# Five of eight pairs of the up projection as products of sums, and low parts by accumulating transfers from HBM, in one encoder layer

## The chip, the cores and the metric

The kernel runs on one core of one Trainium2 chip. The metric is device time in microseconds (us) of one execution. The five engines of the core each run their own list of instructions: TensorE (PE: matmuls, with weight loads shown apart as PEld), VectorE (DVE), ScalarE (ACT), GpSimd (POOL) and SyncE (SP), which here only issues loads. GpSimd issues some transfers too. TensorE writes to PSUM, everything else lives in SBUF, and weights come from HBM by DMA.

## The reference, cut to what matters

One layer of an encoder on 256 tokens of width 2048, all in float32: two kinds of attention side by side with one input and one output projection, cross attention to 256 memory tokens, a SwiGLU with 5632 hidden columns, and a last RMSNorm.

```
h = rms_norm(x, g_mix);   proj = h @ w_in              # MLA and differential attention
x = x + concat([out_mla, out_diff]) @ w_out
x = x + cross_attention(rms_norm(x, g_xattn), rms_norm(mem, g_mem)) @ w_xo
hf = rms_norm(x, g_ffn)
x = x + (silu(hf @ w_gate) * (hf @ w_up)) @ w_down     # w_gate, w_up: 2048 x 5632
return rms_norm(x, g_final)
```

The change concerns the line with `w_gate`, `w_up` and `w_down`.

## The kernel before

**A float32 product as three matmuls.** Each operand is split into a high part (`.h`, the value cast to the reduced type fp32r) and a low part (`.l`, the rest, also fp32r). A product is high × high, high × low and low × high. Of a weight block of 128 × 1024, ScalarE makes the high part by a cast (tile `wh`), and VectorE the low part by a subtract (tile `wl`). Both tiles have rings of four buffers (`w_tile`, L602).

**Pairs.** The depth of a product is taken in pairs of 2 × 128 rows, so hf's 2048 are eight pairs. `wide_project` (L644) computes 256 tokens × 1024 columns: it walks over the pairs in a given order, and for each loads 1 MB of weights into one of three `wraw` buffers (`pair_raw`, L596, issued by SP). A pair has one of two kinds:

- `P`, plain: 2 depths × 2 token halves × 2 column halves × 3 = 24 matmuls of 512 columns, into four accumulators `acc` in PSUM. VectorE makes two low parts of 1024 columns.
- `W`, products of sums (the Strassen–Winograd form for a 2 × 2 block): 7 products × 3 = 21 matmuls, into the accumulators and into four more PSUM banks `q1`, `q5`, `q6`, `q7`. It needs sums of weight blocks, which VectorE writes to the tile `tsum` (one 1024-wide, two 512-wide operations), and the split of each: `b11` and `b21` from `wraw`, `t13` and `t24` from `tsum` (`t24` in single tiles `wh2` and `wl2`). It also needs sums of the activations, the `forms` of `summed_pair` (L627), made once.

`GU_KINDS` (L38) says which pairs are which in gate and up, `G_ORDER` and `U_ORDER` (L46) in which order they are walked.

**Carried low parts.** For a block named in `CARRIED` (L42: pair 0, second block) `split_blocks` (L608) makes the low part without VectorE: ScalarE writes the negated block to `wl`, and the cast to `wh`; then a DMA that GpSimd issues adds the raw block from `wraw` to `wl`.

```
nc.scalar.activation(w.l, src, AF.Copy, scale=-1.0)
nc.scalar.copy(out=w.h, in_=src)
nc.gpsimd.dma_start(out=w.l, in_=src, accum_op=ALU.add)
```

**Stages.** The FFN has a chunk of 512 hidden columns (`narrow_chunk`, L1258) and five wide chunks of 1024 (`wide_chunk`, L1270). A wide chunk is gate by `wide_result`, silu on ScalarE, up by `wide_result`, the multiply on VectorE and the transposes. After the first wide chunk, the third and the fifth stand two down projections each (`wide_add`, L736), whose accumulators start from the residual `x_res`. When the pairs of sums of a down projection are done, `leave` (L744) stores the four sums made of the `q` banks in tiles `left` out of a ring of five (`nat`).

**What sets the order.** The kernel's text only records operations. A planner (`Plan`, L186) with a table of costs (`cost`, L252) puts each engine's operations in an order. In the FFN the matmuls keep the order in which they were recorded (`strict`, L1308 and below), and tiles of the pool `wp` are placed in program order (`Held.queued`, L128). Since one place in the planner emits every operation, all instructions bear the line L232; tiles tell them apart.

Of the kernel before, what the change touches and what calls it, by code (L numbers as in the profile page):

```python
# [10 lines left out]
F32 = mybir.dt.float32  # L11
F32R = mybir.dt.float32r
# [24 lines left out]

GU_KINDS = "PPWPWPWW"  # L38

DN_CARRIED = ((1, 1),)  # L40

CARRIED = ((0, 1),)  # L42

NARROW_KINDS, NARROW_ORDER = "PPWPWPPP", (0, 1, 3, 2, 5, 4, 6, 7)

G_ORDER, U_ORDER = (0, 2, 1, 4, 3, 6, 7, 5), (0, 2, 1, 4, 3, 6, 7, 5)  # L46

# [75 lines left out]
class Held:  # L123


    def __init__(self, pool, shape, args):
        self.pool, self.args, self.real = pool, args, None
        self.queued, self.ahead = pool.name == "wp" and pool.plan.strict, None  # L128
        self.size, self.whole = int(np.prod(shape[1:])), pool.space is not None
        self.ops, self.past, self.opened, self.old, self.end = [], [], [], None, 0.0  # L130
# [329 lines left out]
def encoder_block(tc: tile.TileContext, a, out):  # L460
# [183 lines left out]
    def wide_project(pairs, src, order, kinds, leave, join, closed=(0, 1), before=None, seed=None, carried=()):  # L644
# [6 lines left out]
        for n, i in enumerate(order):  # L651
# [9 lines left out]
            if i not in summed:  # L661
                w = [split_blocks(raw[:, 2 * k:2 * k + 2, :], carried=(i, k) in carried) for k in range(2)]
                for k in range(2):
                    products = []
                    for tt in range(NT):
                        for oc in range(2):

                            ends = stop or i == plain[-1] and tt == oc == 1
                            products.append((accs[tt][oc], pairs[i].at(k, tt), w[k][:, oc, :], not used[tt][oc],
                                             ends and k == 1 and oc in closed))  # L670
                            used[tt][oc] = True
                    mm_late(products, seed is not None)
# [63 lines left out]
    def wide_add(pairs, src, order, kinds, oc0, done=None, closed=(0, 1), before=None, carried=()):  # L736
# [498 lines left out]
    for oc in range(4):  # L1235
# [34 lines left out]
    def wide_chunk(c, kinds):  # L1270

        g = wide_result(x2_pairs, a["w_gate"][c], G_ORDER, GU_KINDS, CARRIED)
# [3 lines left out]
        u = wide_result(x2_pairs, a["w_up"][c], U_ORDER, GU_KINDS, CARRIED)  # L1276
        for oc in range(2):
# [132 lines left out]
def _lay_out(i):  # L1410
# [56 lines left out]
```

## Time and profile before

| | us |
|---|---|
| median of three runs | 1134.45 (1134.06 to 1134.86) |
| the profiled execution | 1134.3 |
| its span in the profile | 1132.5 |
| granted TensorE clock, mean | 0.998 |

The page gives each engine's busy time over the span; the windows view gives it for a stretch. A matmul row's length overlaps the next matmul, so the distance of two starts says more than the length. The groups of VectorE and ScalarE that the change touches, with shapes kept apart; the columns are line, engine, operation, output<-input, shapes, count, busy us, mean ns, idle us before them with what ended it:

```profile
L232 DVE TENSOR_TENSOR wl<-wraw,wh 128x1024 fp32r<-128x1024 f32 x306 | 370.8, 1223 | 72.8 <-ACT wh L232 65.9 <-PE q L232 5.3
L232 DVE TENSOR_TENSOR wl<-tsum,wh 128x1024 fp32r<-128x1024 f32 x112 | 135.2, 1217 | 1.5 <-ACT wh L232 1.4
L232 DVE TENSOR_TENSOR tsum<-tsum,wraw 128x512 f32<-128x512 f32 x124 | 85.0, 685 | 1.4
L232 ACT CAST wh<-wraw 128x1024 fp32r<-128x1024 f32 x321 | 334.9, 1053 | 208.9 <-PE acc L232 176.1 <-issue 12.5 <-PE q L232 5.6
L232 ACT ACTIVATE wl<-wraw 128x1024 fp32r<-128x1024 f32 x15 | 15.9, 1058 | 0.0
```

The last row is the 15 negated blocks of the carried low parts: five chunks, in each one for gate, one for up, and one for each of the five down projections that have them.

### The profile page before, as it was taken

What the parts mean: (1) busy time and instruction counts of PE and PEld (TensorE: products, weight loads), DVE (VectorE), ACT (ScalarE), POOL (GpSimd) and SP (SyncE); (2) the same over time, 40 slices, a digit from 0 to 9 for tenths busy, and PEclk for the clock granted to TensorE, in tenths of its full rate; (3) what the DMA queues carried; (4) which work ended last, traced back from release to release, by engine and by line L of the source; (5) the groups of instructions that cost most, each with busy time, mean ns of one, the idle gap of its engine ahead of it and who ended that gap; (6) DMA issues with size and microseconds to landing.
All of it is one profiled execution on the core that took longest, in us unless ns stands there. A gap on an engine that the chain in (4) does not pass through costs nothing.

```text
span 1132.5 us, 14766 instructions
## 1 busy us (share of the span) xinstructions
PE 1122.3 (99%) x5349; PEld 938.1 (83%) x5349; DVE 1011.5 (89%) x1375; ACT 715.3 (63%) x1014; POOL 72.1 (6%) x90
## 2 busy tenths in 40 slices
PE   9999999999999999999999999999999999999997
PEld 7899888888888888888888888888888888888886
DVE  7798778779997769999998999999989999999995
ACT  7756455467685556666675565767666665766762
POOL 5830000000000000000000000000000000000000
PEclk9999999999999999999999999999999999999999
DMA  9642444547654444666657666576575666667653
GB/s 358 258 166 110 149 149 158 207 167 267 232 211 172 153 169 161 205 216 216 209 204 231 224 217 203 212 232 210 190 236 175 241 224 201 223 218 223 229 184 114
DMA packets 37657, 230.03 MB, mean 203 GB/s; under 512 B 4560, under 2 KB 5840, under 8 KB 13264
## 3 DMA queue, kind: packets, MB, share of 16 engines
q1 hardware_dynamic: 33696, 216.60, 53.5%
q0 software_dynamic: 3024, 11.01, 4.4%
q10 hardware_dynamic: 864, 1.47, 0.4%
q8 instruction: 42, 0.69, 0.3%
q14 instruction: 31, 0.25, 0.1%
HBM read 219.11 MB, written 2.10 MB: 195 GB/s over the span
## 4 chain that ended last, share of the span: by engine, by line
PE 96%; DVE 1%; ACT 1%; issue 1%; POOL 0%; POOLq 0%; DVEq 0%; ACTq 0%
PE acc L232 73%; PE q L232 15%; PE pt L232 2%; PE psc L232 2%; PE acckv L232 1%; PE qT L232 1%; PE po L232 1%; PE kT L232 1%; PE ppt L232 1%; DVE wl L232 0%; PE wps L232 0%; ACT wh L232 0%; PE pod L232 0%; ACT e L232 0%; DVE res L232 0%
## 5 line engine op out<-in xcount | busy, mean ns | idle before, releaser
L232 ACT CAST wh<-wraw 128x1024 fp32r<-128x1024 f32 (+2 forms) x401 | 387.2, 975 | 259.7 <-PE acc L232 217.2
L232 DVE TENSOR_TENSOR wl<-wraw,wh 128x1024 fp32r<-128x1024 f32 (+2 forms) x386 | 430.3, 1125 | 80.6 <-ACT wh L232 72.2
L232 ACT CAST wh<-tsum 128x1024 fp32r<-128x1024 f32 (+1 forms) x124 | 124.2, 1011 | 54.6 <-PE acc L232 35.0
L232 DVE TENSOR_TENSOR wl<-tsum,wh 128x1024 fp32r<-128x1024 f32 (+1 forms) x124 | 143.4, 1166 | 2.2 <-ACT wh L232 1.4
L232 PE MATMUL acc<-wh,x2T_l 128*128 128x512 f32 x352 | 137.2, 390 | 0.0
L232 PE MATMUL acc<-wh,x2T_h 128*128 128x512 f32 x352 | 137.1, 389 | 0.0
L232 PE MATMUL q<-wh,forms_h 128*128 128x512 f32 x242 | 94.8, 392 | 0.6 <-ACT res L232 0.4
L232 PE MATMUL acc<-wl,x2T_h 128*128 128x512 f32 x352 | 94.4, 389 | 0.0
L232 PE MATMUL q<-wh,forms_l 128*128 128x512 f32 x242 | 94.4, 390 | 0.0
L232 PE MATMUL acc<-wh,x0T_h 128*128 128x512 f32 x224 | 88.1, 395 | 0.1
L232 PE MATMUL acc<-wl,x0T_h 128*128 128x512 f32 x224 | 88.1, 394 | 0.0
L232 PE MATMUL acc<-wh,x0T_l 128*128 128x512 f32 x224 | 87.8, 393 | 0.0
L232 DVE TENSOR_TENSOR tsum<-tsum,wraw 128x512 f32<-128x512 f32 x124 | 85.0, 685 | 1.4
L232 PE MATMUL q<-wl,forms_h 128*128 128x512 f32 x242 | 84.1, 389 | 0.0
L232 PE MATMUL acc<-wh,forms_h 128*128 128x512 f32 x208 | 81.2, 391 | 0.0
L232 PE MATMUL acc<-wh,forms_l 128*128 128x512 f32 x208 | 81.0, 389 | 0.0
L232 DVE TENSOR_TENSOR tsum<-wraw 128x1024 f32<-128x1024 f32 (+1 forms) x68 | 76.1, 1124 | 4.4 <-DMA wraw<-in_w_dn 2.2
L232 PE MATMUL acc<-wl,forms_h 128*128 128x512 f32 x208 | 78.2, 390 | 0.0
L232 PEld LDWEIGHTS acc<-wh,x2T_h 128*128 128x128 f32 x352 | 66.1, 188 | 13.7
L232 PEld LDWEIGHTS acc<-wh,x2T_l 128*128 128x128 f32 x352 | 66.1, 188 | 13.6
L232 PEld LDWEIGHTS acc<-wl,x2T_h 128*128 128x128 f32 x352 | 66.0, 188 | 13.6
L232 PE MATMUL acc<-wh,hT_l 128*128 128x512 f32 x188 | 73.4, 390 | 0.0
(363 smaller groups left out, 2095.6 us busy)
## 6 DMA issues: line engine op xcount, KB each, us to landing
wraw<-in_w_dn SPq DMA_DIRECT2D x41, 1024.0 KB, 4.8
wraw<-in_w_gate SPq DMA_DIRECT2D x40, 1024.0 KB, 4.8
wraw<-in_w_up SPq DMA_DIRECT2D x40, 1024.0 KB, 4.8
wraw<-in_w_in SPq DMA_DIRECT2D x24, 1024.0 KB, 4.9
wraw<-in_w_out SPq DMA_DIRECT2D x16, 1024.0 KB, 4.9
wraw<-in_w_gu SPq DMA_DIRECT2D x8, 1024.0 KB, 4.8
wl<-wraw POOLq DMA_DIRECT2D x15, 512.0 KB, 6.8
wraw<-in_w_in_lat SPq DMA_DIRECT2D x5, 832.0 KB, 7.0
```

The source lines that it names most:

```text
L232: getattr(getattr(self.tc.nc, engine), method)(*[made(x) for x in args], **{k: made(x) for k, x in kw.items()})
```

## The change

Each wide chunk gets its own kinds, order and list of carried blocks, the same in all five. Gate keeps four pairs of sums and its order, and carries three low parts instead of one. Up takes pair 3 as sums too, five of eight, walks 0, 2, 3, 1, 4, 6, 7, 5, and carries five low parts. x2, the input of gate and up, has forms for every pair that is `W` in any of them, so for pair 3 also; where a pair is plain, the product uses the plain blocks inside the forms. The last plain pair of x2 (pair 5) lies in tiles `odd` of its own.

A carried low part now lies in a tile `wc` of its own, a ring of two in the pool of the sums, while its high part stays in `wh`. The accumulating DMA reads the block from HBM, not from `wraw`. `tsum` becomes two tiles of two blocks, `tsum` and `tsum2`. The ring of `nat` goes from five to two, and `leave` stores its sums in the columns of the residual. Tiles in PSUM are placed in program order as well. The weights' layout in HBM follows the kinds, chunk by chunk.

```diff
-GU_KINDS = "PPWPWPWW"
...
-CARRIED = ((0, 1),)
...
-G_ORDER, U_ORDER = (0, 2, 1, 4, 3, 6, 7, 5), (0, 2, 1, 4, 3, 6, 7, 5)
+GATE_UP = [
+    (('PPWPWPWW', (0, 2, 1, 4, 3, 6, 7, 5), ((0, 1), (3, 1), (5, 1))),
+     ('PPWWWPWW', (0, 2, 3, 1, 4, 6, 7, 5), ((0, 1), (1, 1), (5, 1), (7, 0), (6, 0)))),
+] * 5
+X2_KINDS = "".join("W" if "W" in k else "P" for k in zip(NARROW_KINDS, *[p[0] for c in GATE_UP for p in c]))
...
-        self.queued, self.ahead = pool.name == "wp" and pool.plan.strict, None
+        self.queued, self.ahead = pool.name in ("wp", "pacc", "pps") and pool.plan.strict, None
...
-    def split_blocks(src, pool=None, carried=False):
-        w = w_tile(src.shape[1], pool)
-        if carried:
+    def split_blocks(src, pool=None, carried=None):
+        w = w_tile(src.shape[1], pool) if carried is None or not sum_pool else Split(
+            wp.tile([P, 1024], F32R, name="wh", tag="wh", bufs=4).rearrange("p (b c) -> p b c", b=2),
+            sum_pool[0].tile([P, 1024], F32R, name="wc", tag="wc", bufs=2).rearrange("p (b c) -> p b c", b=2))
+        if carried is not None:
             nc.scalar.activation(w.l, src, AF.Copy, scale=-1.0)
             nc.scalar.copy(out=w.h, in_=src)
-            nc.gpsimd.dma_start(out=w.l, in_=src, accum_op=ALU.add)
+            nc.gpsimd.dma_start(out=w.l, in_=carried, accum_op=ALU.add)
...
-            b11 = split_blocks(raw[:, 1:3, :], carried=(i, 0) in carried)
+            b11 = split_blocks(raw[:, 1:3, :], carried=src[i][:, 1:3, :] if (i, 0) in carried else None)
             if sum_pool:
-                t = sum_pool[0].tile([P, 4, 512], F32, name="tsum", tag="tsum", bufs=1)
...
+                t = sum_pool[0].tile([P, 2, 512], F32, name="tsum", tag="tsum", bufs=1)
+                v = sum_pool[0].tile([P, 2, 512], F32, name="tsum2", tag="tsum2", bufs=1)
...
         def leave(Q):
             for q in ((0, 0), (1, 0), (0, 1), (1, 1)):
-                sums[q] = nat("left")
+                sums[q] = x(*q)
...
-    nat_pool[:] = wsum, 5
+    nat_pool[:] = wsum, 2
...
-            if not plain and "P" not in GU_KINDS[2 * oc + n + 1:]:
+            if not plain and X2_KINDS[:2 * oc + n + 1].count("P") == X2_KINDS.count("P"):
```

In the list of instructions TensorE has 15 matmuls fewer (5362 to 5347). On VectorE 35 subtracts of 1024 columns from `wraw` go, and 10 subtracts from `tsum`, 5 of 512 columns from `wraw`, 5 sums of 1024 columns and 10 of 512 come; ScalarE has 30 negated blocks more, 10 casts from `tsum` more, 5 casts of 1024 columns from `wraw` fewer and 5 of 512 more; GpSimd has 30 accumulating transfers more (15 to 45); SP issues the same 236 loads in the same order.

TensorE in the up projection of the second wide chunk, pair 3 before; the first half of its 24 matmuls (the second half uses the other block):

```order
L232 MATMUL acc_7012<-wh_7142,x2T_h_4299 128x512
L232 MATMUL acc_7012<-wh_7142,x2T_l_4321 128x512
L232 MATMUL acc_7018<-wh_7142,x2T_h_4299 128x512
L232 MATMUL acc_7018<-wh_7142,x2T_l_4321 128x512
L232 MATMUL acc_7021<-wh_7142,x2T_h_4299 128x512
L232 MATMUL acc_7021<-wh_7142,x2T_l_4321 128x512
L232 MATMUL acc_7027<-wh_7142,x2T_h_4299 128x512
L232 MATMUL acc_7027<-wh_7142,x2T_l_4321 128x512
L232 MATMUL acc_7012<-wl_7155,x2T_h_4299 128x512
L232 MATMUL acc_7018<-wl_7155,x2T_h_4299 128x512
L232 MATMUL acc_7021<-wl_7155,x2T_h_4299 128x512
L232 MATMUL acc_7027<-wl_7155,x2T_h_4299 128x512
```

And now, at the place behind pair 2, the first 12 of its 21 matmuls (`wh_7125` is its block b11, `wh_7153` its sum t13):

```order
L234 MATMUL q1_7130<-wh_7125,forms_h_4278 128x512
L234 MATMUL q1_7130<-wh_7125,forms_l_4287 128x512
L234 MATMUL acc_7086<-wh_7125,forms_h_4278 128x512
L234 MATMUL acc_7086<-wh_7125,forms_l_4287 128x512
L234 MATMUL q1_7130<-wl_7157,forms_h_4278 128x512
L234 MATMUL acc_7086<-wl_7157,forms_h_4278 128x512
L234 MATMUL q5_7144<-wh_7153,forms_h_4278 128x512
L234 MATMUL q5_7144<-wh_7153,forms_l_4287 128x512
L234 MATMUL q7_7147<-wh_7153,forms_h_4278 128x512
L234 MATMUL q7_7147<-wh_7153,forms_l_4287 128x512
L234 MATMUL q5_7144<-wl_7173,forms_h_4278 128x512
L234 MATMUL q7_7147<-wl_7173,forms_h_4278 128x512
```

The pair went from the fifth place, behind pair 4, to the third, behind pair 2, and from the accumulators alone to accumulators and `q` banks.

ScalarE in the same up projection, at its pairs 6, 7 and 5; before:

```order
L232 CAST wh_7167<-wraw_7104 128x1024
L232 CAST wh_7176<-tsum_7148 128x1024
L232 CAST wh2_7188<-tsum_7148 128x1024
L232 CAST wh_7203<-wraw_7104 128x512
L232 CAST wh_7223<-wraw_7137 128x1024
L232 CAST wh_7237<-tsum_7214 128x1024
L232 CAST wh_7249<-wraw_7137 128x512
L232 CAST wh_7258<-wraw_7180 128x1024
L232 CAST wh2_7271<-tsum_7214 128x1024
```

And now (`wc_7230`, `wc_7262` and `wc_7337` are the negated blocks of pairs 6, 7 and 5; `wraw_7191`, `wraw_7209` and `wraw_7276` their raw tiles):

```order
L234 ACTIVATE wc_7230<-wraw_7191 128x1024
L234 CAST wh2_7238<-tsum2_7216 128x1024
L234 CAST wh_7245<-wraw_7136 128x512
L234 CAST wh_7253<-wraw_7191 128x1024
L234 ACTIVATE wc_7262<-wraw_7209 128x1024
L234 CAST wh_7270<-tsum_7257 128x1024
L234 CAST wh_7283<-wraw_7191 128x512
L234 CAST wh_7292<-wraw_7209 128x1024
L234 CAST wh2_7305<-tsum2_7272 128x1024
L234 CAST wh_7314<-tsum_7300 128x1024
L234 CAST wh_7324<-wraw_7209 128x512
L234 ACTIVATE wc_7337<-wraw_7276 128x1024
```

Three negated blocks stand between the casts. The one of pair 7 (`wc_7262`) stands ahead of the cast of pair 6's sum t13 (`wh_7270`), and writes the buffer that the carried part of pair 1 held.

GpSimd's transfers now, from the end of cross attention to the last one of the FFN (before, one row stood in their place, the 15 accumulates from `wraw` to `wl`):

```order
L234 DMA wc<-in_w_gate 128x1024 x3
L234 DMA wc<-in_w_up 128x1024 x5
L234 DMA wc<-in_w_dn 128x1024 x2
L234 DMA wc<-in_w_gate 128x1024 x3
L234 DMA wc<-in_w_up 128x1024 x5
L234 DMA wc<-in_w_gate 128x1024 x3
L234 DMA wc<-in_w_up 128x1024 x5
L234 DMA wc<-in_w_dn 128x1024 x2
L234 DMA wc<-in_w_gate 128x1024 x3
L234 DMA wc<-in_w_up 128x1024 x5
L234 DMA wc<-in_w_gate 128x1024 x3
L234 DMA wc<-in_w_up 128x1024 x5
```

One more to `in_w_dn` follows behind these. All read HBM, three for each gate and five for each up.

More of the change, by code (lines that the diff above doesn't have):

```diff
@@ L661, in wide_project @@
             if i not in summed:
-                w = [split_blocks(raw[:, 2 * k:2 * k + 2, :], carried=(i, k) in carried) for k in range(2)]
+                w = [split_blocks(raw[:, 2 * k:2 * k + 2, :], carried=src[i][:, 2 * k:2 * k + 2, :] if (i, k) in carried else None) for k in range(2)]
                 for k in range(2):
@@ L675, in wide_project @@
                 Q = {q: ps_tile(f"q{q}") for q in (1, 5, 7, 6)}
-            b11 = split_blocks(raw[:, 1:3, :], carried=(i, 0) in carried)
+            b11 = split_blocks(raw[:, 1:3, :], carried=src[i][:, 1:3, :] if (i, 0) in carried else None)
             if sum_pool:
-                t = sum_pool[0].tile([P, 4, 512], F32, name="tsum", tag="tsum", bufs=1)
-                nc.vector.tensor_tensor(out=t[:, 0:2, :], in0=raw[:, 1:3, :],
-                                        in1=raw[:, 0:1, :].to_broadcast([P, 2, 512]), op=ALU.add)
-                t13 = split_blocks(t[:, 0:2, :], carried=(i, 1) in carried)
+                t = sum_pool[0].tile([P, 2, 512], F32, name="tsum", tag="tsum", bufs=1)
+                v = sum_pool[0].tile([P, 2, 512], F32, name="tsum2", tag="tsum2", bufs=1)
+                nc.vector.tensor_tensor(out=t, in0=raw[:, 1:3, :], in1=raw[:, 0:1, :].to_broadcast([P, 2, 512]),
+                                        op=ALU.add)
+                t13 = split_blocks(t)
                 b21 = split_blocks(raw[:, 3:4, :])
-                nc.vector.tensor_tensor(out=t[:, 2, :], in0=t[:, 0, :], in1=raw[:, 2, :], op=ALU.add)
-                nc.vector.tensor_tensor(out=t[:, 3, :], in0=t[:, 2, :], in1=raw[:, 3, :], op=ALU.add)
-                t24 = split_blocks(t[:, 2:4, :], sum_pool[0])
+                nc.vector.tensor_tensor(out=v[:, 0, :], in0=t[:, 0, :], in1=raw[:, 2, :], op=ALU.add)
+                nc.vector.tensor_tensor(out=v[:, 1, :], in0=v[:, 0, :], in1=raw[:, 3, :], op=ALU.add)
+                t24 = split_blocks(v, sum_pool[0])
             else:
@@ L1244, in encoder_block @@
             rows = raw[:, 2 * n:2 * n + 2, :]
-            if GU_KINDS[2 * oc + n] == "W":
+            if X2_KINDS[2 * oc + n] == "W":
                 x2_pairs.append(summed_pair(rows[:, :, :P], rows[:, :, P:]))
                 continue
-            if not plain and "P" not in GU_KINDS[2 * oc + n + 1:]:
+            if not plain and X2_KINDS[:2 * oc + n + 1].count("P") == X2_KINDS.count("P"):
                 plain = [Split(*[wsum.tile([P, 2, S], F32R, name="odd" + x, tag="odd" + x, bufs=1) for x in "hl"])]
@@ L1270, in wide_chunk @@
     def wide_chunk(c, kinds):
-        g = wide_result(x2_pairs, a["w_gate"][c], G_ORDER, GU_KINDS, CARRIED)
+        g = wide_result(x2_pairs, a["w_gate"][c], GATE_UP[c][0][1], GATE_UP[c][0][0], GATE_UP[c][0][2])
         for oc in range(2):
@@ L1275, in wide_chunk @@
                 nc.scalar.activation(g[tt][:, oc, :], g[tt][:, oc, :], AF.Silu, scale=rstdf[:, tt:tt + 1])
-        u = wide_result(x2_pairs, a["w_up"][c], U_ORDER, GU_KINDS, CARRIED)
+        u = wide_result(x2_pairs, a["w_up"][c], GATE_UP[c][1][1], GATE_UP[c][1][0], GATE_UP[c][1][2])
         for oc in range(2):
@@ L1443, in _lay_out @@
         "w_gu0": _pairs(np.concatenate([i["w_gate"][0][:, :512], i["w_up"][0][:, :512]], axis=1), NARROW_KINDS)[0],
-        "w_gate": _pairs(i["w_gate"][0][:, 512:], GU_KINDS),
-        "w_up": _pairs(i["w_up"][0][:, 512:], GU_KINDS),
+        "w_gate": np.concatenate([_pairs(i["w_gate"][0][:, 512 + 1024 * c:1536 + 1024 * c], GATE_UP[c][0][0]) for c in range(NPC)]),
+        "w_up": np.concatenate([_pairs(i["w_up"][0][:, 512 + 1024 * c:1536 + 1024 * c], GATE_UP[c][1][0]) for c in range(NPC)]),
         "w_dn": np.concatenate([_pairs(i["w_down"][0][:, :1024], DN_KINDS), _pairs(i["w_down"][0][:, 1024:], DN_LAST)]),
```

## The prediction, on record before the run

> **What bounds the kernel now.** I read the head of the page and its chain of waits first, then the windows, because a share over the whole span hides stages. In the windows view the columns are: stretch, length, busy time of PE, PEld, DVE, ACT and POOL with instruction counts, granted clock, DMA share, GB/s.
>
> ```profile
> span 1132.5 us, 14766 instructions
> PE 1122.3 (99%) x5349; PEld 938.1 (83%) x5349; DVE 1011.5 (89%) x1375; ACT 715.3 (63%) x1014; POOL 72.1 (6%) x90
> PE 96%; DVE 1%; ACT 1%; issue 1%; POOL 0%; POOLq 0%; DVEq 0%; ACTq 0%
> ...
> 750.00:780.00 30.00, 30.00 (x134) 24.82 (x134) 29.92 (x37) 19.86 (x23) 0.00 (x0) 1.00 0.65 232
> 665.66:706.46 40.80, 40.80 (x182) 33.78 (x180) 39.05 (x44) 26.16 (x29) 0.86 (x1) 1.00 0.66 220
> 746.90:787.60 40.70, 40.70 (x181) 33.72 (x180) 40.47 (x50) 27.93 (x34) 0.00 (x0) 1.00 0.61 211
> 480.00:1080.00 600.00, 599.44 (x2682) 495.50 (x2681) 578.47 (x687) 394.88 (x468) 13.15 (x16) 1.00 0.64 216
> ...
> PE wps L232 <- DVE warm L232: 1.2, 1, 1.2
> PE po L232 <- ACT e L232: 0.5, 1, 0.5
> PE q L232 <- ACT res L232: 0.4, 2, 0.2
> PE po L232 <- ACT val_h L232: 0.2, 1, 0.2
> ```
>
> The reader is to see three things. From 480 to 1080 us, which is the FFN, TensorE is busy 599.44 of 600 us, and all its waits in the last four rows come to 2.3 us, none of them on a weight or a transfer. So a matmul taken out of this stage is time taken off the end, as long as its operands still arrive. Second, VectorE is hardly less full: 40.47 of 40.70 us in the up stage of the second wide chunk (row 746.90), 578.47 of 600 overall. It is a second bound that keeps pace by a hair. Third, the DMA engines stand at 0.61 to 0.66 in the two up stages.
>
> **What one matmul is worth.** PE's timeline (start, length, engine, line, operation) of up's pair 3, which the change turns from plain into sums, and of a pair that is sums already:
>
> ```profile
> 767.29 0.39 PE L232 MATMUL acc<-wh,x2T_h 128*128 128x512 f32 x1
> ...
> 772.73 0.39 PE L232 MATMUL q<-wh,forms_h 128*128 128x512 f32 x1
> ...
> 668.38 0.39 PE L232 MATMUL q<-wh,forms_h 128*128 128x512 f32 x1
> ...
> 673.14 0.39 PE L232 MATMUL acc<-wh,x2T_h 128*128 128x512 f32 x1
> ```
>
> The 24 matmuls of the plain pair take 772.73 − 767.29 = 5.44 us, 0.2267 each; the 21 of the pair of sums take 673.14 − 668.38 = 4.76 us, again 0.2267. The 0.39 us of a row is its length with overlap, not its price. So a pair gives 3 × 0.2267 = 0.68 us, and five chunks with one such pair each give 15 × 0.2267 = **3.40 us**.
> The Trainium skill ("TensorE: Matmul & The Clock Gate", section "Wait — 56ns, not 53.3ns?") has 215.7 ns from start to start for warm 512-column matmuls; by that the term would be an estimate of 15 × 0.2157 = 3.24 us. The rows have 0.2267 at a granted clock of 1.00, so the measurement decides.
>
> **VectorE.** Its timeline in a pair of sums:
>
> ```profile
> 669.55 1.22 DVE L232 TENSOR_TENSOR wl<-wraw,wh 128x1024 fp32r<-128x1024 f32 x1
> 670.68 1.22 DVE L232 TENSOR_TENSOR tsum<-wraw 128x1024 f32<-128x1024 f32 x1
> 671.82 1.22 DVE L232 TENSOR_TENSOR wl<-wraw,wh 128x1024 fp32r<-128x1024 f32 x1
> 672.96 0.68 DVE L232 TENSOR_TENSOR tsum<-tsum,wraw 128x512 f32<-128x512 f32 x1
> 673.56 1.22 DVE L232 TENSOR_TENSOR wl<-wraw,wh 128x1024 fp32r<-128x1024 f32 x1
> ...
> 694.65 1.22 DVE L232 TENSOR_TENSOR wl<-tsum,wh 128x1024 fp32r<-128x1024 f32 x1
> ```
>
> Start to start a 1024-wide operation costs 1.135 us, a 512-wide one 0.60. A plain pair has two subtracts, 2.27 us. A pair of sums has four 1024-wide operations (three low parts, one sum) and three 512-wide ones: 4 × 1.135 + 3 × 0.60 = 6.34 us. So up's pair 3 costs VectorE 4.07 us more a chunk. Against it, each newly carried low part takes one 1.135 us subtract away: four more in up (4.54), two more in gate (2.27). Up comes to −0.47 us a chunk, gate to −2.27, together −2.74, or −13.7 over five. VectorE isn't the end, so I count this as nothing. It is the cover of the main term: without the carried parts up would need 40.47 + 4.07 = 44.5 us of VectorE for 40.0 us of TensorE, 4.5 us late a chunk. With them it is 40.0 against 40.0, and gate carries the slack over. Locally pairs 2 and 3 now follow each other: 2 × 6.34 − 2 × 4.76 = 3.16 us of VectorE's lead go there. The last row above ends at 695.87 and TensorE first uses it at 697.85 (quoted next): a lead of 1.98 us, the shortest that I found in these stages. Pair 0 before them has one subtract (1.135 us for 5.44 us of TensorE) and rebuilds 4.3 us, and so does pair 1 behind them; I take the cover to hold. The additional forms of x2's pair 3 are eight small operations once, under 2 us, between the cross attention and the FFN; VectorE's other work there decides, and I count 0 (bound: 2 us).
>
> **ScalarE, GpSimd and the transfers.** For each carried part ScalarE writes the negated block beside the cast, GpSimd issues the accumulate:
>
> ```profile
> 656.45 1.06 ACT L232 ACTIVATE wl<-wraw 128x1024 fp32r<-128x1024 f32 x1
> 657.41 1.03 ACT L232 CAST wh<-wraw 128x1024 fp32r<-128x1024 f32 x1
> ...
> 657.80 0.86 POOL L232 DMA_DIRECT2D wl<-wraw  x1 [39.94 <-ACT wl L232]
> ...
> 667.47 1.07 PE L232 MATMUL acc<-wl,x2T_h 128*128 128x512 f32 x4
> ...
> 697.85 0.39 PE L232 MATMUL q<-wl,forms_h 128*128 128x512 f32 x1
> ...
> wraw<-in_w_up SPq DMA_DIRECT2D x40, 1024.0 KB, 4.8
> ...
> wl<-wraw POOLq DMA_DIRECT2D x15, 512.0 KB, 6.8
> ...
> mn<-in_mem POOLq DMA_DIRECT2D x4, 512.0 KB, 4.1
> ...
> DMA to landing us min/median/max: 4.5/6.8/8.9
> ...
> q1 hardware_dynamic: 1152, 8.39, 58.1%
> ...
> wraw<-in_w_dn SPq DMA_DIRECT2D x3, 1024.0 KB, 6.9
> gfb<-in_g_final POOLq DMA_DIRECT2D x2, 512.0 KB, 8.0
> ...
> q0 software_dynamic: 3024, 11.01, 4.4%
> ```
>
> ScalarE's step is 657.41 − 656.45 = 0.96 us; up gets four more and, for the sums, one 1024-wide and one 512-wide cast (about 1.5 us): 27.93 + 5.3 = 33.2 of 40.0 us. GpSimd gets 30 more issues of 0.86 us, 25.8 us on an engine that is 6% busy. Both are hidden: 0. What gives way if they aren't is ScalarE at pairs 6 and 7: three 1024-wide casts, a 512-wide one and a negation, near 4.6 of 4.76 us.
>
> The transfers are the price that is not shown. Before, the accumulate read the raw tile on the chip; now it reads HBM, once more for bytes that were loaded already. I take the 6.8 us from issue to landing, since it is the same form and size from another source; the bounds are the 4.5 and 8.9 of the tile's view (the row with min, median and max). The queue's share in the second up stage, 58.1% of 40.70 us for eight loads, gives 2.96 us of the 16 engines a load. The 21 transfers of GpSimd (15 accumulates, 4 and 2 plain ones of the same size) took 4.4% of 1132.5 us, 2.4 us each. Up would then hold 8 × 2.96 + 5 × 2.4 = 35.7 of 40.0 us, a share of 0.89 against 0.66 before.
> The Trainium skill ("Perfetto Trace Analysis", section "Identifying the Most-Contended Engine") holds busy time misleading for DMA because of the 16 engines, and wants the bandwidth. By bytes up would move 8.39 + 5 × 0.52 = 11.0 MB in 40.0 us, 275 GB/s against the 211 of row 746.90; no run so far shows where such a mixture saturates, so I keep a case for each reading.
>
> **The new wait.** The low parts have a ring of two. In up the fourth (pair 7) reuses the second (pair 1), whose last matmul stands 47 starts before the first use of the new one: 47 × 0.2267 = 10.65 us. Off go the end of the matmul (0.39), ScalarE's write (1.06) and 0.29 until GpSimd issues (the write quoted above ends at 657.51, the issue stands at 657.80): 8.9 us are left for the landing, 2.1 more than 6.8. Before, that part was first used at 667.47, 2.9 us after a landing at 657.80 + 6.8. Queued behind the waiting write on ScalarE are the casts of pair 6's second block, which have 28 starts, 6.35 us, less 0.39, 1.06 and 1.05: 3.8 us to spare. On GpSimd only further accumulates stand behind. The other carried parts have 2.6 us or more beyond 6.8. So the wait costs 0, and loses the pair's 0.68 us only when the landing of pair 7 comes to 8.9 + 0.68 = 9.6 us on the average of the chunks. A wait that goes:
>
> ```profile
> SPq L232 <- DVE wl L232: 815.1, 173, 28.4
> SPq L232 <- DMA wl<-wraw: 116.3, 15, 9.5
> ...
> L232 DVE TENSOR_TENSOR left<-q,left 128x512 f32<-128x512 f32 x24 | 16.5, 688 | 0.5
> ```
>
> SP's next load no longer waits for an accumulate to have read the raw tile (116.3 us in 15 times). Next late is VectorE or ScalarE reading the same tile, which is what it waits for 173 times anyway. A load that is issued earlier has no one waiting for it: 0. The down projections' stored sums, now in the residual's columns, and the order in which accumulators are placed add no instruction; the columns were read when the accumulators were seeded, pairs before. 0 as well; a late seed would hold the four writes behind it, 0.69 us each by the row below, at most 2.8 us once a down projection.
>
> **Sum.** The profiled execution took 1134.3 us, 1132.5 of span and 1.8 around it; the median is 1134.45, so both agree to 0.15 us. 1134.3 − 3.4 = 1130.9; with the median 1131.05. I say **1131.0 us**.
>
> **Rivals.**
> *The carried parts land late (slower).* If pair 7's transfer gets the longest landing seen and one more transfer ahead of it, 8.9 + 2.4 = 11.3 us, TensorE waits 2.4 us a chunk: −3.4 + 5 × 2.4 = +8.6, 1142.9 us. It decides from 9.6 us. For it: loads took 6.9 us and GpSimd's 8.0 where both queues were full (the window of 1035 to 1050, rows gfb and in_w_dn), against 4.8 else; and three accumulates and three loads fall on pairs 6, 7 and 5, 3 × (2.4 + 2.96) = 16.1 us of transfers for 66 matmuls, 15.0 us. Against it: 2.1 us in hand at the median. 0.19.
> *The loads come late and VectorE's lead is eaten (no change).* Loads at 6.9 instead of 4.8 us start VectorE 2.1 us later in a stage in which it has no slack; past the 1.98 us of lead, 0.1 to 0.7 us are lost at two places (pairs 2 and 3, pairs 6 and 7) in five chunks: 1 to 7 us, 1131.9 to 1137.9, about 1134.5 in the middle. The Trainium skill ("DMA: Bandwidth & Descriptors", section "Issuing engines are not separate DMA queues") states that transfers of all issuers share the 16 engines and interleave; the 6.9 and 8.0 agree. Against it: raw tiles come free earlier, and carried parts give VectorE 4.3 us back at three pairs of up. 0.25.
> *A matmul is worth its row.* If the pairs are worth the 0.39 us shown, 15 × 0.39 = 5.85, 1128.4 us. The two timelines speak against it. 0.02.
> *The change doesn't do what it says:* 15 matmuls fewer is counted in the order of the instructions; no chance of its own.
>
> **How the numbers follow.** 0.2% (2.27 us) is about what a measurement of this kernel tells from no change. The forecast, 0.54, has its own range of 1130.0 to 1132.2 (from 0.9 us under the sum, should earlier loads or VectorE's freed 13.7 us give anything, to a loss of 0.25 us a chunk). Faster is the forecast, the third rival and the 0.04 of the second that ends under 1132.2, together 0.60. Of the rest of the second 0.17 is no change, and its last 0.04, over 1136.7, goes with the first rival's 0.19 into slower, 0.23. The range must leave out at most 2 in 10: from 1129.8 (only the third rival lies below) to 1139.0, which holds the second rival whole and the first where it has barely begun.
>
> **What would show it.** TensorE has 15 matmuls fewer, and its window over an up stage is 40.0 us with busy time equal to its length. Among PE's waits a row for a transfer of the carried tile would be the first rival, a row for VectorE's low parts the second. The landing of the carried transfers should have a median under 7.5 and not pass 8.9; loads in up a median near 4.8. VectorE's share in gate should fall by 2.3 us a chunk. I'm wrong if the landings pass 9.6 us on the average, or if VectorE is behind at pair 3.

## The result, and the profile after

| | us | ratio to before, 95% interval |
|---|---|---|
| before, median | 1134.49 (1134.06 to 1134.86) | |
| after, median of 4 runs | 1161.14 (1157.95 to 1163.07) | 1.0232 [1.0209, 1.0256] |
| after, profiled execution | 1161.12, span 1159.0 | |

The change makes the kernel 26.6 us slower; 1131.0 was forecast. TensorE has 15 matmuls fewer, as forecast (x5349 to x5334 in the page). The page of the profile after, first its head, its chain of waits and GpSimd's queue of transfers (packets, MB, share of 16 engines), then transfers (count, size, median us from issue to landing):

```profile
span 1159.0 us, 14748 instructions
PE 1130.6 (98%) x5334; PEld 934.3 (81%) x5334; DVE 1000.7 (86%) x1376; ACT 746.7 (64%) x1056; POOL 98.1 (8%) x120
...
q0 software_dynamic: 7344, 26.74, 12.7%
...
PE 65%; DMA 11%; DVE 11%; issue 6%; ACT 3%; POOL 3%; SPq 0%; POOLq 0%; ACTq 0%; DVEq 0%
...
wraw<-in_w_up SPq DMA_DIRECT2D x40, 1024.0 KB, 6.7
...
wc<-in_w_up POOLq DMA_DIRECT2D x25, 512.0 KB, 8.7
...
wc<-in_w_gate POOLq DMA_DIRECT2D x15, 512.0 KB, 7.7
...
DMA to landing us min/median/max: 5.4/7.8/12.2
```

TensorE fell from 96% to 65% of the chain; transfers and VectorE took 11% each. VectorE's own busy time fell, as forecast. What is new is in the lower rows: a weight load takes 6.7 us to land where it took 4.8, and the carried parts take up to 12.2 (last row, the view of the tile `wc`).

What TensorE waited for, and the windows of the five up stages (from their first matmul to that of the next stage; 40.80 us each before), then of a short stretch in the third:

```profile
PE q L234 <- DMA wc<-in_w_up: 9.1, 5, 2.0
PE acc L234 <- DMA wc<-in_w_up: 3.1, 2, 1.6
PE q L234 <- DVE wl L234: 2.5, 5, 0.5
PE acc L234 <- DMA wc<-in_w_gate: 1.2, 1, 1.2
...
517.13:562.46 45.33, 42.16 (x179) 32.61 (x177) 40.66 (x47) 31.71 (x39) 3.45 (x4) 1.00 0.83 236
668.25:714.48 46.23, 42.70 (x179) 32.39 (x177) 41.13 (x48) 30.63 (x36) 4.31 (x5) 1.00 0.81 233
759.03:803.40 44.37, 42.34 (x179) 34.20 (x178) 39.91 (x50) 34.53 (x42) 4.31 (x5) 0.96 0.82 235
929.07:974.70 45.63, 41.81 (x178) 32.76 (x177) 40.47 (x46) 33.69 (x38) 4.31 (x5) 1.00 0.82 241
1017.89:1063.74 45.85, 42.32 (x179) 34.21 (x178) 41.05 (x51) 35.22 (x43) 5.42 (x7) 0.96 0.81 231
786.00:790.00 4.00, 4.00 (x18) 3.00 (x16) 3.93 (x8) 2.13 (x4) 0.00 (x0) 1.00 1.03 295
```

The up stages have grown to 45.33, 46.23, 44.37, 45.63 and 45.85 us. That is 227.4 against 5 × 40.80 = 204.0, so 23.4 of the 26.5 us of span. With 177 matmuls instead of 180 each they would take 40.12 without waits, 200.6 in all, so 26.8 us are lost there. The DMA share stands at 0.81 to 0.83 for a whole stage and at 1.03 around 788 us (a packet counts whole where it starts, so a short window can pass 1).

Two places show the two kinds of loss. The first is pair 7 of up: GpSimd's issues and TensorE's timeline in the third stage.

```profile
777.28 0.86 POOL L234 DMA_DIRECT2D wc<-in_w_up  x1 [12.43 <-ACT wc L234]
781.09 0.86 POOL L234 DMA_DIRECT2D wc<-in_w_up  x1 [2.94 <-ACT wc L234]
...
789.63 0.39 PE L234 MATMUL acc<-wh,forms_l 128*128 128x512 f32 x1
792.02 0.50 PE L234 MATMUL q<-wc,forms_h 128*128 128x512 f32 x1 [2.00 <-DMA wc<-in_w_up]
...
793.40 0.63 PE L234 MATMUL q<-wh,forms_h 128*128 128x512 f32 x1
793.83 0.63 PE L234 MATMUL q<-wh,forms_l 128*128 128x512 f32 x1
```

Pair 7's transfer is issued at 781.09, and TensorE would have used it at 789.86, one matmul after 789.63: 8.8 us for the landing, the 8.9 of the prediction. It landed only just before 792.02, after 10.9 us, so the matmul starts 2.2 us late (the 2.00 in its row counts from the end of the row before). Pair 6's transfer was issued 3.8 us ahead of it. In the five chunks pair 7's landing took 10.6, 11.1, 10.9, 9.9 and 10.3 us. Behind this wait the matmuls start 0.43 us apart (793.40, 793.83) instead of 0.23, at half the granted clock (the last section has its rows).

The second place is the start of up in the first chunk, on VectorE, after and before (the bracket is idle time ahead and what ended it):

```profile
514.04 1.23 DVE L234 TENSOR_TENSOR tsum<-wraw 128x1024 f32<-128x1024 f32 x1 [4.77 <-DMA wraw<-in_w_up]
515.19 1.41 DVE L234 TENSOR_TENSOR res<-q,res 128x512 f32<-128x512 f32 x2
...
517.96 1.22 DVE L234 TENSOR_TENSOR wl<-wraw,wh 128x1024 fp32r<-128x1024 f32 x1
```

```profile
509.62 2.36 DVE L232 TENSOR_TENSOR wl<-wraw,wh 128x1024 fp32r<-128x1024 f32 x2 [0.61 <-PE q L232]
511.90 1.41 DVE L232 TENSOR_TENSOR res<-q,res 128x512 f32<-128x512 f32 x2
```

Before, VectorE spent these us on low parts of gate's last pair and of up's first, and then on gate's results. Now one low part of gate's last pair is carried as well, and next in VectorE's order stands pair 2's sum (514.04). So it is idle for 4.77 us until pair 2's load lands: that was issued at 506.64 and took 7.3 us (before: 506.06 and 4.8). For the last 2.3 us of that, work was ready: gate's matmuls into the `q` banks and ScalarE's cast for pair 0 were done by 511.7. But in VectorE's order gate's results (`res<-q`, `res<-acc`) and even pair 0's own low part (517.96) stand behind the sum; TensorE takes that low part up at 519.23, 0.3 us late. From there on the results are mixed with the sums of pairs 2 and 3, and TensorE waits for those. By the first matmuls of the pairs this is 0.8 us at pair 2 and 1.6 at pair 3 in the first two chunks.

Adding up every start in the FFN that comes over 0.05 us later than a matmul's price: first uses of carried parts about 15 us (0.4 in kernels that don't wait for them), of VectorE's low parts 6 (0.4 before), of high parts 3 (2.4), and the matmuls right behind a wait or at the lower clock 8 (0.4); where one draws the lines moves each by up to 1.5. Together they give 31.9, against 3.3 before: 28.6 us lost, of which the fewer matmuls give back 3.4. About 1.1 of the 26.5 us lie in starts that are late by less than 0.05.

### The profile page after: what moved, and what is told of

Same layout as the page of the kernel before. It is cut to its first block, busy times and chain, and to the rows that moved or that the text cites. A ratio compares the mean times of both kernels' runs of the same rounds, so it can differ in the third digit from the quotient of the medians.

```text
span 1159.0 us, 14748 instructions
## 1 busy us (share of the span) xinstructions
PE 1130.6 (98%) x5334; PEld 934.3 (81%) x5334; DVE 1000.7 (86%) x1376; ACT 746.7 (64%) x1056; POOL 98.1 (8%) x120
## 4 chain that ended last, share of the span: by engine, by line
PE 65%; DMA 11%; DVE 11%; issue 6%; ACT 3%; POOL 3%; SPq 0%; POOLq 0%; ACTq 0%; DVEq 0%
PE acc L234 49%; PE q L234 9%; DVE wl L234 5%; DMA wc<-in_w_up 5%; DMA wraw<-in_w_up 4%; DVE tsum L234 3%; PE pt L234 2%; PE psc L234 2%; ACT wh L234 2%; DVE res L234 1%; POOL prod L234 1%; PE qT L234 1%; DMA wraw<-in_w_dn 1%; DMA wc<-in_w_gate 1%; PE po L234 1%
## 5 line engine op out<-in xcount | busy, mean ns | idle before, releaser
L234 DVE TENSOR_TENSOR wl<-wraw,wh 128x1024 fp32r<-128x1024 f32 (+2 forms) x356 | 391.8, 1110 | 89.1 <-ACT wh L234 86.9
L234 DVE TENSOR_TENSOR wl<-tsum,wh 128x1024 fp32r<-128x1024 f32 (+1 forms) x134 | 156.1, 1171 | 8.2 <-ACT wh L234 7.2
L234 PE MATMUL acc<-wh,forms_h 128*128 128x512 f32 x271 | 106.4, 392 | 0.0
L234 PE MATMUL acc<-wh,forms_l 128*128 128x512 f32 x271 | 106.0, 391 | 0.0
L234 PE MATMUL acc<-wh,hT_h 128*128 128x512 f32 x188 | 73.4, 391 | 0.0
L234 PE MATMUL acc<-wh,x2T_h 128*128 128x512 f32 x176 | 69.0, 392 | 0.0
L234 PE MATMUL acc<-wh,x2T_l 128*128 128x512 f32 x176 | 68.7, 391 | 0.0
L234 ACT ACTIVATE wc<-wraw 128x1024 fp32r<-128x1024 f32 x45 | 47.6, 1059 | 32.5 <-DMA wraw<-in_w_up 16.5
L234 PEld LDWEIGHTS acc<-wh,forms_l 128*128 128x128 f32 x271 | 51.2, 189 | 11.2 <-DVE forms_l L234 0.8
L234 PEld LDWEIGHTS q<-wh,forms_h 128*128 128x128 f32 x262 | 49.5, 189 | 13.1 <-ACT res L234 1.3
```

Source lines behind the costliest of these rows:

```text
L234: getattr(getattr(self.tc.nc, engine), method)(*[made(x) for x in args], **{k: made(x) for k, x in kw.items()})
```

## The experiments

**Theory T:** the accumulating transfers crowd the DMA engines; they land late, the loads beside them land late, and the engines that work in order pass it on. **Rivals:** S, the new places and the source in HBM cost, not the number; V, VectorE (with the sums of pairs 2 and 3 side by side) is late of itself; H, reading HBM twice is what crowds; N, only the number counts; O, the order of the instructions is bad.

Unless said otherwise an experiment is the changed kernel with another table. The lines are gate's kinds, order and carried parts, and up's.

### The old table in the new code

```diff
-    (('PPWPWPWW', (0, 2, 1, 4, 3, 6, 7, 5), ((0, 1), (3, 1), (5, 1))),
-     ('PPWWWPWW', (0, 2, 3, 1, 4, 6, 7, 5), ((0, 1), (1, 1), (5, 1), (7, 0), (6, 0)))),
+    (('PPWPWPWW', (0, 2, 1, 4, 3, 6, 7, 5), ((0, 1),)),
+     ('PPWPWPWW', (0, 2, 1, 4, 3, 6, 7, 5), ((0, 1),))),
```

> The changed kernel with the old table: four pairs of sums in up, one carried low part each in gate and up, in the old order. What stays of the change: the tiles wc in a ring of two, the accumulates from HBM, the shorter ring nat, PSUM tiles in program order. Theory T (the 30 additional accumulates crowd the 16 DMA engines: they wait for one another and the loads for them): about the time before, 1133.5 to 1136, landings of wc 6 to 8 us, loads in up 4.8 us. Rival S (the new places and the source in HBM are what costs, not the number): 1142 or more, with a row of PE's waits for wc.

1134.55 us, ratio 1.0001 [0.9991, 1.0010]. S is out: tiles of their own, a ring of two, the shorter `nat` and a source in HBM cost nothing while there are 15 accumulates.

### The carried parts alone, and the sums alone

```diff
-     ('PPWWWPWW', (0, 2, 3, 1, 4, 6, 7, 5), ((0, 1), (1, 1), (5, 1), (7, 0), (6, 0)))),
+     ('PPWPWPWW', (0, 2, 1, 4, 3, 6, 7, 5), ((0, 1), (1, 1), (5, 1), (7, 0), (6, 0)))),
```

> The changed kernel with the old kinds and order in up (four pairs of sums), but all the new carried parts, three in gate, five in up. VectorE has 4.07 us a chunk less to do than in the changed kernel, TensorE 0.68 us more. Theory T: the transfers stay late, pair 7's landing about 10 us, loads in up near 6.7 us; the waits for VectorE go, those for wc stay: 1134.5 + 15 to 20, so 1148 to 1155. Rival V (VectorE, late by the sums of pairs 2 and 3, is the main loss and only delays the transfers): 1133 to 1137.

1146.40 us, 1.0101 [1.0084, 1.0118], below the 1148 to 1155 of T and far above V. Landings and loads stay late (the profiled execution took 1149.27):

```profile
wraw<-in_w_up SPq DMA_DIRECT2D x40, 1024.0 KB, 6.7
wc<-in_w_up POOLq DMA_DIRECT2D x25, 512.0 KB, 8.5
...
PE q L234 <- DMA wc<-in_w_up: 6.0, 4, 2.0
```

The carried parts by themselves, with less work for VectorE, lose 11.7 us. And the sums by themselves:

```diff
-    (('PPWPWPWW', (0, 2, 1, 4, 3, 6, 7, 5), ((0, 1), (3, 1), (5, 1))),
-     ('PPWWWPWW', (0, 2, 3, 1, 4, 6, 7, 5), ((0, 1), (1, 1), (5, 1), (7, 0), (6, 0)))),
+    (('PPWPWPWW', (0, 2, 1, 4, 3, 6, 7, 5), ((0, 1),)),
+     ('PPWWWPWW', (0, 2, 3, 1, 4, 6, 7, 5), ((0, 1),))),
```

> The changed kernel's sums and order in up, but only one carried part each in gate and up, as before. TensorE saves 3.4 us in all; VectorE has 4.07 us a chunk more in up and no relief. Theory T: no crowding, landings of wc 6 to 8 us, loads near 4.9 us; TensorE waits for VectorE's low parts by most of the 4.07 a chunk less what slack it had: 1137 to 1151. Rival V (VectorE's place, not the transfers, made most of the changed kernel's loss): above 1155.

1150.90 us, 1.0142 [1.0127, 1.0158], at the upper end of T's range. In its rows the loads are at their old 4.8 us, and the waits are for VectorE and for ScalarE (which waits behind it):

```profile
wraw<-in_w_up SPq DMA_DIRECT2D x40, 1024.0 KB, 4.8
...
PE q L234 <- DVE wl L234: 3.9, 8, 0.9
PE q L234 <- ACT wh L234: 3.7, 4, 1.2
```

So the cover was needed (16.4 us above before, with 3.4 saved: 19.8 lost, 4.0 a chunk, as large as the 4.07 of additional work and near the 4.5 that the prediction gave), and the cover that was chosen costs more than it covers.

### Without the carried parts of pairs 6 and 7

```diff
-     ('PPWWWPWW', (0, 2, 3, 1, 4, 6, 7, 5), ((0, 1), (1, 1), (5, 1), (7, 0), (6, 0)))),
+     ('PPWWWPWW', (0, 2, 3, 1, 4, 6, 7, 5), ((0, 1), (1, 1), (5, 1)))),
```

> The changed kernel without the carried parts of pairs 6 and 7 in up, which VectorE subtracts again: 1.135 us twice a chunk more on VectorE. Theory T: PE's waits for wc go nearly whole and loads in up come back to about 5.5 us; VectorE has 42.3 us of work for 40.0 in up, with gate's 2.3 us of slack behind it, so up to 2 us a chunk are lost there: 1131 to 1143. Rival V: VectorE's lateness grows by what it has more, 2.3 us a chunk and more: 1165 or above.

1142.79 us, 1.0071 [1.0056, 1.0086]. TensorE has no wait for `wc` any more, though VectorE does 2.27 us a chunk more: giving ten transfers back to VectorE gains 18 us. Most of the waits that are left are for VectorE's low parts (5.1 us), with loads in up at 5.9 us; how much of that is VectorE's own work and how much late loads isn't separated here.

### The accumulates from the raw tile

```diff
-            nc.gpsimd.dma_start(out=w.l, in_=carried, accum_op=ALU.add)
+            nc.gpsimd.dma_start(out=w.l, in_=src, accum_op=ALU.add)
```

> The changed kernel, but its accumulates read the raw tile on the chip as before the change, not HBM. Theory T: the accumulates still write and read as many bytes through the same engines, pair 7's landing stays near 10 us, and the loads wait for raw tiles that the accumulates hold besides: 1155 to 1170. Rival H (the second reading of HBM is the load that crowds the engines): 1131 to 1145, landings of 7 us, loads of 4.8 to 5 us.

1152.32 us, 1.0167 [1.0139, 1.0194], below T's range and above H's. The median landing fell to 6.0 us, loads in up only to 6.3. Pair 7's own landing stayed at 10.0 to 10.8 us, as T had it, and TensorE still waited there in every chunk:

```profile
wc<-wraw POOLq DMA_DIRECT2D x45, 512.0 KB, 6.0
...
PE q L234 <- DMA wc<-wraw: 10.0, 5, 2.4
```

Reading HBM again is worth about 9 of the 26.6 us; two thirds stay.

### Four carried parts, spread and close

Old kinds and order, gate with one carried part; the first spreads up's four over the stage, the second has three of them in a row.

```diff
+     ('PPWPWPWW', (0, 2, 1, 4, 3, 6, 7, 5), ((0, 1), (1, 1), (3, 1), (7, 0)))),
```

> The old kinds and order; gate carries one part, up four, that lie about ten us apart (pairs 0, 1, 3 and 7). VectorE is relieved of 3 subtracts a chunk. Theory T in its narrow form (an accumulate lands late when another one was issued shortly before): landings 6 to 8 us, no wait of TensorE for wc, 1133.5 to 1137. Rival N (the number of accumulates crowds the engines wherever they lie): as the kernel with four close ones, 1140 or more.

```diff
+     ('PPWPWPWW', (0, 2, 1, 4, 3, 6, 7, 5), ((0, 1), (6, 0), (7, 0), (5, 1)))),
```

> As the kernel with four spread ones, same number and same relief of VectorE, but the carried parts of up are those of pairs 0, 6, 7 and 5. Theory T in its narrow form: pair 7's landing 9.5 to 11 us with a wait of TensorE for wc of about 1 us a chunk or more: 1138 to 1146. Rival N: the same time as the spread ones, within 2 us.

A miss, and a useful one: the spread ones took 1148.44 us, 1.0128 [1.0111, 1.0145], the close ones 1137.72, 1.0026 [1.0017, 1.0036]. Neither N (same number, 10.7 us apart) nor T in its narrow form (neighbours delay each other) holds. Spread (first fence) and close (second):

```profile
wraw<-in_w_up SPq DMA_DIRECT2D x40, 1024.0 KB, 6.8
wc<-in_w_up POOLq DMA_DIRECT2D x20, 512.0 KB, 6.4
...
PE acc L234 <- DVE hT_l L234: 4.3, 2, 3.2
PE q L234 <- ACT res L234: 3.8, 2, 2.1
```

```profile
wraw<-in_w_up SPq DMA_DIRECT2D x40, 1024.0 KB, 5.3
wc<-in_w_up POOLq DMA_DIRECT2D x20, 512.0 KB, 7.6
```

Spread, each accumulate lands soon (6.4), but the loads in up take 6.8 us; close, the accumulates delay one another (7.6) and the loads are at 5.3. And the spread kernel loses its time at the changes of stages, in TensorE's waits for `hT_l` and `res`, where VectorE and ScalarE put one stage's results away and prepare the next.

### The same instructions, short transfers

Each accumulate adds 128 of its 1024 columns, so these kernels leave out seven eighths of each addend and don't compute the layer; every engine has the same instructions in the same order. First the changed kernel:

```diff
-            nc.gpsimd.dma_start(out=w.l, in_=carried, accum_op=ALU.add)
+            nc.gpsimd.dma_start(out=w.l[:, 0:1, :128], in_=carried[:, 0:1, :128], accum_op=ALU.add)
```

> The changed kernel, instruction for instruction in the same order, but each accumulate moves only an eighth of its block (128 of 1024 columns), so most of each carried low part lacks its addend. Theory T (the bytes of the accumulates crowd the DMA engines; landings and loads are late, and everything behind them): landings of wc 3 to 5 us, loads near 4.8 us, no wait of TensorE for wc, 1130.5 to 1133, near the 1131 forecast. Rival V (VectorE's and ScalarE's work, or the order of the instructions, is late by itself): 1140 or more, with waits for VectorE at up's pairs 2 and 3.

1132.51 us, 0.9982 [0.9973, 0.9991]. Its rows of transfers, its waits of TensorE, and the windows of the first and third up stage:

```profile
wraw<-in_w_up SPq DMA_DIRECT2D x40, 1024.0 KB, 4.9
...
wc<-in_w_up POOLq DMA_DIRECT2D x25, 64.0 KB, 2.8
...
PE q L234 <- ACT res L234: 0.6, 2, 0.4
...
516.69:556.82 40.13, 40.13 (x178) 33.18 (x177) 38.41 (x44) 33.13 (x40) 3.45 (x4) 1.00 0.65 218
745.53:785.65 40.12, 40.12 (x178) 33.23 (x177) 39.31 (x50) 33.85 (x41) 4.32 (x5) 1.00 0.58 192
```

This decides. With all of VectorE's, ScalarE's and GpSimd's work in place and only the bytes taken away, the loads are at 4.9 us, no wait for `wc` or for a low part is left, and the up stages take 40.13 and 40.12 us (40.12 to 40.37 over all five) against the forecast's 40.0. The bytes of the accumulates cost 28.6 us. V is out for the changed kernel: its order of work does no harm when the transfers are short. The spread kernel, made short in the same way:

> The kernel with four spread carried parts, same order, accumulates an eighth as long. It took 1148.4 us, which the narrow theory (only neighbours hurt each other) did not have. Theory T in its wide form (each accumulate delays the load beside it, from 4.8 to 6.8 us, and in-order engines pass that on to the change of stages): 1133.5 to 1136. Rival O (the planner's order of that kernel is bad at the change of stages, with or without transfers): 1143 or more.

1136.44 us, 1.0016 [1.0007, 1.0025]: 12.0 of the spread kernel's 14.0 us went with the bytes, 2 stayed. So T in its wide form holds there as well, and O has a small part.

### Versions made from this

Up's sums with carried parts at pairs 0, 3, 4 and 7, and gate's at 0 and 3:

```diff
+    (('PPWPWPWW', (0, 2, 1, 4, 3, 6, 7, 5), ((0, 1), (3, 1))),
+     ('PPWWWPWW', (0, 2, 3, 1, 4, 6, 7, 5), ((0, 1), (3, 0), (4, 0), (7, 0)))),
```

> The changed kernel's sums and order, with carried parts spread: up's pairs 0, 3, 4 and 7, gate's 0 and 3. VectorE: up +4.07 - 3 x 1.135 = +0.67 us a chunk, gate -1.135. Theory T: landings below 8.5 us, no wait for wc at pair 7; VectorE's lateness at the start of up, where it waits for pair 2's load and has gate's results to put away, stays in part: 1131 to 1138. Rival N: 1145 or more.

1135.91 us, 1.0015 [1.0005, 1.0024]. The up stages take 40.1 to 40.5 us; lost again are 1.0 to 1.3 us at gate's first pair in two chunks (waits for `wc<-in_w_gate`) and 2.0 at the last change to the down projection. The same with one carried part in gate:

```diff
-    (('PPWPWPWW', (0, 2, 1, 4, 3, 6, 7, 5), ((0, 1), (3, 1))),
+    (('PPWPWPWW', (0, 2, 1, 4, 3, 6, 7, 5), ((3, 1),)),
```

> The sums in up with up's carried parts at pairs 0, 3, 4 and 7, but gate carries only pair 3's, not pair 0's, whose landing of 10.6 us at the change from up to gate held TensorE up by 1.0 to 1.3 us in two chunks. VectorE has 1.135 us a chunk more in gate. Theory T: those two waits go, 1132 to 1135. Rival V: VectorE, with one subtract more, is late instead, 1137 or more.

A miss for T: 1137.63 us, 1.0034 [1.0022, 1.0047], in V's range. Those two waits went, but in the profiled execution (1140.59) others came for ScalarE's `res` and `hT_h` (2.4 us each) at the changes of stages; whether VectorE, with its subtract more, is behind them isn't shown. The first of these tables with the accumulates from the raw tile (`in_=src` for `in_=carried`, as above):

> The sums in up with spread carried parts (pairs 0, 3, 4, 7; gate 0, 3), accumulates from the raw tile instead of HBM. With HBM it took 1135.9 us. From the changed kernel to its form from the raw tile the time fell by 9 us, landings from 7.8 to 6.0 us. Theory T: landings near 6 us and loads below 5.4, so 1131 to 1134.5. Rival (raw tiles that are held longer delay the loads as much): 1136 or more.

A miss: 1135.83 us, 1.0008 [0.9999, 1.0017]. Up is at its 40.12 us in four of five chunks, but the last down projections take 74.1 us against 69.9. There, from 1030 to 1060 us, the transfers of the last gain (`gfb`) lie among the loads:

```profile
wraw<-in_w_dn SPq DMA_DIRECT2D x5, 1024.0 KB, 8.2
gfb<-in_g_final POOLq DMA_DIRECT2D x2, 512.0 KB, 9.8
```

So their issue was moved behind the first of the last two down projections, with the raw tile as source and with HBM:

```diff
-        gfb = [act.tile([P, 1024], F32, name="gfb", tag="act") for _ in range(2)]
-        for c in range(2):
-            load = nc.gpsimd.dma_start(out=gfb[c], in_=a["g_final"][:, c * 1024:(c + 1) * 1024].partition_broadcast(P))
-            load.after(last_split[0], False)
...
         wide_add(hp, src[0], order, kinds, 0, final_square, carried=[x for x in DN_CARRIED if x[0] < len(kinds) and kinds[x[0]] == "P"])
+        gfb = [act.tile([P, 1024], F32, name="gfb", tag="act") for _ in range(2)]
...
```

> The sums with spread carried parts from the raw tile (it took 1135.8 us, and its up stages all took 40.12 us), with one thing more: the two 512 KB loads of the last gain, which fell on the change from the last up to the last down projection beside loads that took 8 to 11 us, are issued behind the first of the last two down projections. Theory T: that change loses its 4 us (74.1 us for the down projection against 69.9 before), so 1131 to 1133: the sums' 3.4 us are to be had when the transfers are eased. Rival (VectorE's and ScalarE's order at that change is late by itself, not by transfers): 1135 to 1137.

> The same table and the same late gain loads, but accumulates from HBM as in the changed kernel. Theory T: gate's first pair of chunks 2 and 4 still waits for its part (1.0 to 1.3 us each), the last change is better by about 2 us: 1132.5 to 1135.5, above the form from the raw tile. Rival: the same time as the form from the raw tile within 0.5 us, the source doesn't matter.

1134.52 us, 1.0000 [0.9991, 1.0009], and 1135.83, 1.0009 [1.0000, 1.0018]. From the raw tile the last down projections came down to 71.4 us: 2.7 of the 4.2 us were the gain's transfers. The expected 1131 to 1133 was missed all the same: in the profiled execution (1133.64) by what is left there and 0.4 us each in one gate and one up. The second lies just above T's 1132.5 to 1135.5 and is further from the first than the rival's 0.5: HBM as the source is 1.3 us slower by the medians with 35 accumulates, but the intervals overlap, so this isn't settled. No version that computes everything beats the kernel before beyond the measurement.

## Why the prediction was wrong

- **Main term, 3.40 us for 15 matmuls:** right in the stages. Up takes 40.12 us where nothing is late. In the time of the kernel with short transfers it shows as 2.2 us (1134.68 to 1132.51; by the interval 1.0 to 3.1), in the spans of the profiled executions as 2.9 (1132.5 to 1129.6), with 0.6 us more of late starts than before.
- **VectorE's sum:** near as a sum (busy 1011.5 to 1000.7 us, 10.8 less, where 13.7 less up to 2 us of new forms were worked out), and so was the need for cover: without it the sums lose 4.0 us a chunk where 4.5 were worked out.
- **The step that failed is that the transfers were counted as 0, by their landing:** "I take the 6.8 us from issue to landing, since it is the same form and size from another source". Form and size were the same, the company wasn't. The budget of 8.9 us was about right (8.8 in the chunk shown, 8.1 to 9.1 over the five), but pair 7's transfer took 9.9 to 11.1 us. The prediction had worked out the reason, a share of 0.89 in up (0.82 over the lengthened stage) and 16.1 us of transfers for 15.0 us of matmuls at pairs 6, 7 and 5, and still kept the median of a time when an accumulate met no other. By its own rival, "it decides from 9.6 us"; that was passed in every chunk. What stood in place of the 0: with the same instructions and the transfers shortened to an eighth the kernel took 1132.51 us, so their bytes cost 28.6 us.
- **The price of an accumulate was too small as well:** the 2.4 us of the 16 engines are a mean of 15 accumulates with 6 plain transfers. The accumulates alone took 2.7 us each before (from the raw tile) and 3.1 now (from HBM), worked out at the end. With 3.1 the prediction's own sum is 8 × 2.96 + 5 × 3.1 = 39.2 of 40.0 us, and 18.2 for pairs 6, 7 and 5: by this nothing was in hand. Measured, the share of 0.81 to 0.83 of the lengthened stages is 36 to 38 us.
- **The rival's price was too small:** 2.4 us a chunk at one place, 8.6 us in all. The place was right and the wait there (1.7 to 2.2 us) near it, but it left out pair 5 (1.7 to 1.8 us in two chunks), gate's first pair (1.4 in one), the lower clock behind long waits, and the loads, which the second rival had apart, as if only one of the two could come. They come together, from the same bytes.
- **Pair 0 as a source of lead** ("has one subtract ... and rebuilds 4.3 us"): wrong. VectorE takes its work in order and can't run ahead of a raw tile that hasn't landed; it stood idle for 4.77 us there, with work behind the sum that waited. And gate's eight results, 512 wide, fall on pairs 0 to 2 of up; they were in the stage's sum but not in that of the pairs.
- **"A load that is issued earlier has no one waiting for it: 0"**: the freed raw tiles did gain nothing, since the load that mattered was issued at about the same time and landed later: 4.8 us became 6.7.
- **The bandwidth rule** of the Trainium skill ("Perfetto Trace Analysis", section "Identifying the Most-Contended Engine"), quoted in the prediction, would have read the stage as hardly fuller than before: 231 to 241 GB/s in up, against 232 in a stretch of before in which nothing waited. Here the busy share told better: 0.61 to 0.66 without loss, 0.81 to 0.83 with it.
- **A reading:** the up stage of row 746.90 is that of the third wide chunk, and row 665.66 begins 2.7 us into that of the second (662.94 to 703.74). All five take 40.80 us, so no term depends on it.

What stays open: how the 28.6 us divide between late carried parts and late loads (the count by first uses puts about 15 on the first, directly); what a third buffer for `wc`, or pair 0's low part ahead of pair 2's sum on VectorE, would have saved, since no run has either; and why the close carried parts hurt the changes of stages less than the spread ones; only that bytes make up 12.0 of the spread ones' 14.0 us is shown.

## What to carry to other kernels

An idle issuing queue does not make a transfer free. Add up the DMA engines' time by stage, and by pairs where the new transfers fall together, with a price taken from transfers of that kind alone. When the sum nears the stage's length, take landing times from a place in the trace with that company. A test that keeps every instruction and its order and only shortens the transfers separates bytes from work in one run. The lead of an engine that works in order is limited by buffers that have landed, so work taken off it in front of a late load is no gain, and work that is ready is no help when it stands behind the one that waits.

## What the runs showed of the hardware

- TensorE's granted clock fell to half behind some of its long waits. Matmuls then started 0.43 us apart, about 0.2 us more each for eight of them, so the wait at 792.02 cost 1.6 us beyond itself. In the changed kernel this happened behind two of the five waits at pair 7, of 2.2 us each, not behind the others (2.0 us or less); with the carried parts alone it came after a late start of 2.13 us and not after another of 2.17. Each stretch at half clock inside the FFN, in every trace, lasts 3.41 us or twice that, and begins a whole number of 3.41 us after the clock's first rise. What tells the cases apart is how long TensorE was busy in the window of that grid just before. Two windows of the changed kernel, each with the one behind it (busy PE is the first number behind the comma, the clock stands third from the end):

```profile
789.21:792.62 3.41, 1.41 (x7) 0.86 (x6) 2.86 (x7) 2.78 (x4) 0.86 (x1) 1.00 0.97 358
792.62:796.03 3.41, 3.41 (x10) 2.63 (x9) 1.43 (x3) 3.00 (x4) 0.00 (x0) 0.50 0.86 195
550.28:553.69 3.41, 1.68 (x8) 1.09 (x7) 1.27 (x2) 3.12 (x4) 0.86 (x1) 1.00 0.97 310
553.70:557.11 3.41, 3.41 (x17) 2.80 (x16) 2.44 (x3) 3.41 (x6) 0.00 (x0) 1.00 0.92 150
```

  Over all 16 traces every window at full clock with at most 1.54 us of busy PE was followed by half clock, none with 1.70 us or more; between them lie 1.68 (not) and 1.69 (yes). The wait of 2.17 us fell across the border of two windows, the first of which kept 1.97 us busy. The Trainium skill ("TensorE: Matmul & The Clock Gate", section "What's actually happening") ties the clock to activity in a window of about 3.4 us that runs freely. The traces agree, with 3.41 us.
- An accumulating transfer of 512 KB took more than a plain one. GpSimd's queue held only accumulates from 465 to 1030 us before (14, 6.6% of 565 us: 2.7 us of the 16 engines each, from the raw tile) and from 463 to 1030 us now (41, 22.3% of 567 us: 3.1 us, from HBM). Four plain transfers of the same size (`mn`, 240 to 310 us before) took 7.9% of 70 us, 1.4 us each, and a plain load of 1 MB 2.96. The 3.1 us are no effect of the crowd: with the sums alone, and 14 accumulates from 460 to 1040 us, it is 7.4% of 580 us, again 3.1.
